# Order of the four TensorE products in a unit of two feature blocks: high, low, high, low or high, high, low, low

## The chip, the cores and the metric

The kernel runs on one core of a Trainium2 chip. The metric is the device time of one execution in microseconds (us). A core has a matrix engine (TensorE, PE in the profile, with its weight loads listed as PEld), a vector engine (DVE), a scalar engine (ACT), GpSimd (POOL) and a queue engine (SP) that issues the transfers from HBM. PE writes its results into PSUM, which has banks of 512 fp32 values in each of 128 partitions.

## The reference, cut to what matters

Two layers act on 256 tokens of width 1024. Each layer is a SwiGLU block, a token mixer, and a second SwiGLU block:

```python
def swiglu(h, w_gate_up, w_down):
    a, b = jnp.split(h @ w_gate_up, 2, axis=-1)      # 1024 -> 2 x 2816
    return (jax.nn.silu(a) * b) @ w_down             # 2816 -> 1024

x = x + 0.5 * swiglu(rms_norm(x, ffn1_norm), ffn1_w_gate_up, ffn1_w_down)
h = rms_norm(x, mix_norm)
z = h @ w_in                                         # u, q, k, v and two gate logits of 1024
...                                                  # pooling, attention in one block of 256 positions
gates = jax.nn.sigmoid(gl + b_gate).reshape(B, S, N_BRANCH, D)
merged = gates[:, :, 0] * (y_pool @ w_branch_pool) + gates[:, :, 1] * (y_attn @ w_branch_attn)
x = x + merged @ w_out
x = x + 0.5 * swiglu(rms_norm(x, ffn2_norm), ffn2_w_gate_up, ffn2_w_down)
```

All of it is float32. What the change touches are the products `h @ w_gate_up` (four times) and the gate logits (twice).

## The kernel before, in words

**Split operands.** A float32 number is held as two float32r parts, a high one and a low one (the rest). A product of activations and weights is formed from three part products: weight-high by activation-high, weight-high by activation-low, and weight-low by activation-high. Activations lie features by tokens: `hx` has, for each block `k` of 128 features, a tile `hk[k]` of 128 x 2 x 256, whose first 256 columns are the high part and whose second 256 the low part. A block of weights is 128 x 128. So one matmul with a high weight block streams 512 columns (both parts, `prod` with `xk`), and one with a low weight block streams 256 (the high part alone, `xk[:, 0, :]`). Below, H is the first kind and L the second. Each matmul has its own weight load. `steps` only sets the order in which the columns of a matmul run.

**Weights.** They come from HBM in units of 128 x 2048 fp32 (16 blocks of 128 x 128, 1 MB), by `unit()`: SP issues the transfer into one of four `raw` buffers, ACT writes the high part (line 112) and DVE the low part (line 113), each in two halves of 8 blocks, into `hi` and `lo` tiles (six halves of each). ACT may overwrite a half when the matmuls that read it are done.

**A unit of two feature blocks.** `pair` makes two blocks of 128 output features (`j` = 0, 1) from one unit: `columns` runs over the eight blocks `k` of the contraction, and for each over `j`. The sums of `j` = 0 and `j` = 1 lie in two PSUM banks: `banks` gives a tile of 2 x 2 x 256 fp32 in each partition, and `ps[:, j]` is one bank of it, with the H product in both halves and the L product added onto the first half. For the first three units `pairs` runs the same `columns` in turns over pieces of `k`, one of the units with two `quarter` tiles in place of one `banks` tile (that is the list that `ps` can be). Two such `banks` tiles are in use by turns; `drain` adds the halves into SBUF (ACT, line 158, then DVE, line 159).

**Who calls it.** `ffn` calls `pair` (or `pairs`, or `columns` itself, in the first units) for the 22 units of `w_gate_up`, four times in all, and `gate` calls it for 8 units of gate logits in each of the two layers. That is 4 x 22 + 2 x 8 = 104 units of 8 blocks of `k`, 832 turns of the loop over `k`, and 1664 of H and as many of L. `chain` itself is also called by `project_u` and by the second half of `ffn` (the products by `w_down`, tiles `ga` and `gb`), one bank at a time; there its order is H, L, H, L. `tokens` (tile `pt`) alternates H and L as well, with activations as weights. `chain3`, in the mixer's later products and the last block of the output, uses matmuls of 256 columns alone: two with the high block and one with the low.

**Order.** All matmuls are kept in the order in which the program lists them (`keep`). The order within the other engines' queues is that of the program too.

Of the kernel before, what the change touches and what calls it, by code (L numbers as in the profile page):

```python
# [29 lines left out]
NK = D // P  # L30
# [19 lines left out]
def trunk_kernel(ctx: ExitStack, tc: tile.TileContext, x_in, w_in, pw_in, qkn_in, rope_in, mask_in, band_in, out):  # L50
# [28 lines left out]
    def mm(*args, **kw):  # L79
        return keep(nc.tensor.matmul(*args, **kw))  # L80
# [34 lines left out]
    def blk(z, b, n=1):  # L115

        c = b * P % HALF
        return z[b * P // HALF][:, c:c + n * P]

    def steps(z):  # L120

        if len(z.shape) == 3:
            z = z.rearrange("p a s -> p (a s)")
        return z.rearrange("p (s a c) -> p a s c", a=4, c=4)

    def prod(ps, w, xk, first, last):

        return mm(steps(ps), lhsT=w, rhs=steps(xk), start=first, stop=last)

    def chain(ps, hi, lo, b, xk, first, last):  # L130

        prod(ps, blk(hi, b), xk, first, False)
        return prod(ps[:, 0, :], blk(lo, b), xk[:, 0, :], False, last)
# [7 lines left out]

    def columns(w, ps, ks):

        for k in ks:
            for j in range(2):
                chain(ps[j] if isinstance(ps, list) else ps[:, j], *w, 2 * k + j, hk[k], k == 0, k == NK - 1)

    def pair(w, t, other=None, at=0):

        ps = banks(pmm, "ps")  # L150
        columns(w, ps, range(at))
        if other:
            other()
        columns(w, ps, range(at, NK))
        drain(t, ps)
# [5 lines left out]
    def pairs(ws, ts):  # L161

        pss = [banks(pmm, "ps"), banks(pmm, "ps"), [quarter("pe") for _ in range(2)]]
        for a, b in PIECES:
            for w, ps in zip(ws, pss):
                columns(w, ps, range(a, b))
        for t, ps in zip(ts[:2], pss):
            drain(t, ps)
        for j, pe in enumerate(pss[2]):
            act(ts[2][:, j, :], pe[:, 1, :], AF.Copy)  # L170
            tt(ts[2][:, j, :], pe[:, 0, :], ts[2][:, j, :], op=OP.add)
# [35 lines left out]
    hk = [hx[:, k] for k in range(NK)]  # L207
# [545 lines left out]
```

## Time and profile before

| what | value |
|---|---|
| runs | 1010.97 us median of 3 (1008.93, 1010.97, 1013.57) |
| profiled execution | span 1008.4 us from the first to the last instruction; no other time is given for it |
| PE busy | 1001.3 us, 99% of the span, 6348 matmuls and as many weight loads |
| PEld busy | 905.9 us |
| DVE busy | 795.9 us |
| ACT busy | 626.1 us |
| granted PE clock | 1.000 |

The profile has a page with the busy time of each engine, the chain of work that ended last and the costliest groups of instructions, and it can be asked for a timeline, for waits, and for groups in a window. "ps<-hx,hi" is a matmul that writes a tile `ps` from `hx` with a block of `hi`: an H of a unit of two feature blocks. A matmul's recorded duration (383 ns for 512 columns) includes the time to the end of its last write, while the next one has begun: for the rate of a row of matmuls the distance of the starts is read, not the duration.

### The profile page before, as it was taken

The numbers are of one execution on the slowest core, as the hardware profiler recorded it, in microseconds if no ns is written. First come the engines' busy times: TensorE is split into PE (matmuls) and PEld (weight loads), VectorE is DVE, ScalarE is ACT, GpSimd is POOL, SyncE is SP. The second block draws the span as 40 slices with busy tenths as digits, with TensorE's granted clock in tenths as the row PEclk, the third lists the DMA queues.
The fourth block names the chain that finished last, engine by engine and source line by source line (L and its number), as shares of the span: only waits on it lengthen the run. The fifth ranks groups of instructions, "written<-read, shape, count | busy, mean of one in ns | idle before, by whom it ended". The sixth has DMA issues, their size and how long they took to land.

```text
span 1008.4 us, 16031 instructions
## 1 busy us (share of the span) xinstructions
PE 1001.3 (99%) x6348; PEld 905.9 (90%) x6348; DVE 795.9 (79%) x1195; ACT 626.1 (62%) x985; POOL 1.4 (0%) x26
## 2 busy tenths in 40 slices
PE   8999999999999999999999999999999999999998
PEld 7889889898899998898898898898988998989987
DVE  7898866699769788886678888666998798888752
ACT  7966655567766766665576666556676567665641
POOL 0000000000000000000000000000000000000000
PEclk9999999999999999999999999999999999999999
DMA  8766566545526566656646565655544375656640
GB/s 290 272 229 218 180 209 209 192 156 169 204 84 227 192 209 209 209 174 206 206 168 211 206 209 175 207 203 186 189 167 147 118 255 173 228 181 209 207 148 22
DMA packets 30459, 192.91 MB, mean 191 GB/s; under 512 B 3376, under 2 KB 5680, under 8 KB 7856
## 3 DMA queue, kind: packets, MB, share of 16 engines
q1 hardware_dynamic: 30240, 191.71, 55.8%
q8 instruction: 50, 0.82, 0.3%
q10 hardware_dynamic: 144, 0.18, 0.1%
q14 instruction: 25, 0.20, 0.1%
HBM read 190.82 MB, written 1.05 MB: 190 GB/s over the span
## 4 chain that ended last, share of the span: by engine, by line
PE 84%; DVE 9%; ACT 3%; issue 2%; DMA 1%; SPq 0%; ACTq 0%; DVEq 0%
PE ps L80 73%; PE pt L80 6%; PE two L80 4%; DVE lo L113 3%; ACT hi L112 1%; DMA raw<-w 1%; DVE gates L159 1%; ACT pr L427 1%; DVE gates L483 1%; DVE nb L422 1%; DVE pr L432 1%; DVE sc L417 0%; ACT gates L486 0%; DVE gates L514 0%; DVE ab L322 0%
## 5 line engine op out<-in xcount | busy, mean ns | idle before, releaser
L80 PE MATMUL ps<-hx,hi 128*128 128x512 f32 x1712 | 574.8, 383 | 2.1 <-ACT hi L112 1.1
L113 DVE TENSOR_TENSOR lo<-raw,hi 128x1024 fp32r<-128x1024 f32 (+2 forms) x369 | 440.2, 1196 | 128.5 <-ACT hi L112 123.2
L112 ACT ACTIVATE hi<-raw 128x1024 fp32r<-128x1024 f32 (+2 forms) x369 | 379.3, 1035 | 219.0 <-PE ps L80 172.2
L80 PE MATMUL ps<-hx,lo 128*128 128x256 f32 x1712 | 467.8, 273 | 0.2 <-DVE lo L113 0.2
L80 PEld LDWEIGHTS ps<-hx,hi 128*128 128x128 f32 x1712 | 321.4, 188 | 60.9 <-DVE ab L159 1.7
L80 PEld LDWEIGHTS ps<-hx,lo 128*128 128x128 f32 x1712 | 321.7, 188 | 0.7 <-DVE lo L113 0.5
L80 PE MATMUL ps<-ga,hi 128*128 128x512 f32 (+1 forms) x528 | 172.4, 376 | 0.0
L80 PE MATMUL ps<-ga,lo 128*128 128x256 f32 x512 | 139.8, 273 | 0.0
L80 PEld LDWEIGHTS ps<-ga,hi 128*128 128x128 f32 x528 | 97.9, 188 | 16.6
L80 PEld LDWEIGHTS ps<-ga,lo 128*128 128x128 f32 x512 | 96.2, 188 | 0.0
L80 PE MATMUL ps<-gb,hi 128*128 128x512 f32 (+1 forms) x198 | 65.6, 376 | 0.0
L80 PE MATMUL pt<-hi,hx 128*128 128x512 f32 x192 | 65.1, 385 | 0.0
L322 DVE TENSOR_TENSOR ab<-ab,r 128x512 f32<-128x512 f32 x88 | 60.5, 691 | 2.4
L159 DVE TENSOR_TENSOR ab<-ps,ab 128x512 f32<-128x512 f32 x87 | 59.8, 687 | 2.2
L324 ACT ACTIVATE sg<-ab 128x256 f32<-128x256 f32 x88 | 36.6, 418 | 30.6 <-DVE ab L322 29.8
L80 PE MATMUL pt<-lo,hx 128*128 128x256 f32 x192 | 52.6, 274 | 0.0
L80 PE MATMUL ps<-gb,lo 128*128 128x256 f32 x192 | 52.4, 273 | 0.0
L158 ACT ACTIVATE ab<-ps 128x512 f32<-128x512 f32 x87 | 50.5, 580 | 0.3 <-PE ps L80 0.3
L175 ACT ACTIVATE ga<-sg 128x256 fp32r<-128x256 f32 x64 | 26.3, 418 | 36.4 <-DVE sg L325 35.2
L80 PE MATMUL two<-ax,hi 128*128 128x256 f32 x256 | 44.9, 278 | 0.1
L80 PE MATMUL ps<-ax,hi 128*128 128x256 f32 x256 | 44.1, 275 | 0.0
L80 PEld LDWEIGHTS ps<-gb,hi 128*128 128x128 f32 x198 | 36.7, 188 | 6.2
(148 smaller groups left out, 856.3 us busy)
## 6 DMA issues: line engine op xcount, KB each, us to landing
raw<-w SPq DMA_DIRECT2D x176, 1024.0 KB, 5.0
raw<-w SPq DMA_DIRECT2D x9, 256.0 KB, 6.2
raw<-w SPq DMA_DIRECT2D x2, 512.0 KB, 6.3
out_dram<-gx SPq DMA_DIRECT2D x8, 128.0 KB, 2.0
raw<-w SPq DMA_DIRECT2D x6, 128.0 KB, 3.7
gx<-x SPq DMA_DIRECT2D x3, 256.0 KB, 6.0
qk<-pw SPq DMA_DIRECT2D x2, 256.0 KB, 2.7
qkn<-qkn SPq DMA_DIRECT2D x1, 256.0 KB, 5.4
```

Of the source, the lines that this page charges most:

```text
L80: return keep(nc.tensor.matmul(*args, **kw))
L112: act(hi, w, AF.Copy)
L113: tt(lo, w, hi.bitcast(F32), op=OP.subtract)
L158: act(t, ps[:, :, 1, :], AF.Copy)
L159: tt(t, ps[:, :, 0, :], t, op=OP.add)
L175: act(d[:, 0, :], v, AF.Copy)
L322: tt(ab, ab, bc2(r[0]), op=OP.mult)
L324: act(sg, ab[:, 0, :], AF.Silu)
L422: nc.vector.tensor_reduce(nb[:, j, :], sc[:, :, c], axis=AX.X, op=OP.max)
L427: act(pr[:, h, c], sc[:, h, c], AF.Exp, scale=DH ** -0.5, bias=nb[:, j, h:h + 1], accum_out=su[:, j, h:h + 1])
L432: tt(pr[:, :, c], pr[:, :, c], su[:, j, :].unsqueeze(2).to_broadcast([P, 2, n]), op=OP.mult)
L483: tt(gates[:, f], gates[:, f], bc2(r), op=OP.mult)
```

## The change

In `columns` alone, the four matmuls of a block `k` change their order. Before: H of `j` = 0, L of `j` = 0, H of `j` = 1, L of `j` = 1. After: H of `j` = 0, H of `j` = 1, L of `j` = 0, L of `j` = 1. So two H follow each other, then two L, and every matmul writes to the other bank than the one before it. The number of matmuls, weight loads, their shapes and operands stay the same; `start` and `stop` flags stay on the same matmuls (the first H and the last L of each bank).

```diff
     def columns(w, ps, ks):
 
+        hi, lo = w
+        pj = ps if isinstance(ps, list) else [ps[:, j] for j in range(2)]
         for k in ks:
             for j in range(2):
-                chain(ps[j] if isinstance(ps, list) else ps[:, j], *w, 2 * k + j, hk[k], k == 0, k == NK - 1)
+                prod(pj[j], blk(hi, 2 * k + j), hk[k], k == 0, False)
+            for j in range(2):
+                prod(pj[j][:, 0, :], blk(lo, 2 * k + j), hk[k][:, 0, :], False, k == NK - 1)
```

## The prediction

> **What bounds the kernel now.** I read the page first: span, busy shares, the chain of work that ended last, the costliest groups.
>
> ```profile
> span 1008.4 us, 16031 instructions
> ...
> PE 1001.3 (99%) x6348; PEld 905.9 (90%) x6348; DVE 795.9 (79%) x1195; ACT 626.1 (62%) x985; POOL 1.4 (0%) x26
> ...
> PEclk9999999999999999999999999999999999999999
> ...
> PE 84%; DVE 9%; ACT 3%; issue 2%; DMA 1%; SPq 0%; ACTq 0%; DVEq 0%
> ...
> L80 PE MATMUL ps<-hx,hi 128*128 128x512 f32 x1712 | 574.8, 383 | 2.1 <-ACT hi L112 1.1
> ...
> L80 PE MATMUL ps<-hx,lo 128*128 128x256 f32 x1712 | 467.8, 273 | 0.2 <-DVE lo L113 0.2
> ```
>
> PE is busy nearly all the time, at full granted clock, and makes up 84% of the chain. The busy time says little of its rate, since matmuls overlap: the two bottom rows hold H (512 columns) and L (256 columns), 383 and 273 ns long each. Their idle time, 2.1 and 0.2 us in all, says that PE hardly waits for anybody. So the kernel lasts as long as its matmuls need at their rate, and the change touches that rate alone. Hence I read the chain in order of time for rates over long stretches, and the timeline for single starts.
>
> ```profile
> 46.57 139.22 PE ps L80 x832
> 185.79 10.96 PE pt L80 x64
> ...
> 208.21 10.68 PE pt L80 x64
> ...
> 339.11 176.00 PE ps L80 x1056
> ```
>
> Columns: start in us, length in us, what, count. 176.00 us for 1056 matmuls, H and L by turns, is 333.3 ns for an H and an L together. This stretch holds both the units of two blocks and the products by `w_down`. Before 46.57 us the chain runs through DMA, ACT and DVE too; after it, nearly all is PE. The two `pt` rows come in below.
>
> ```profile
> 500.17 0.28 PE L80 MATMUL ps<-ga,lo 128*128 128x256 f32 x1
> 500.28 0.38 PE L80 MATMUL ps<-ga,hi 128*128 128x512 f32 x1
> 500.50 0.27 PE L80 MATMUL ps<-ga,lo 128*128 128x256 f32 x1
> 500.61 0.38 PE L80 MATMUL ps<-ga,hi 128*128 128x512 f32 x1
> 500.83 0.28 PE L80 MATMUL ps<-ga,lo 128*128 128x256 f32 x1
> ...
> 500.17 0.19 PEld L80 LDWEIGHTS ps<-ga,hi 128*128 128x128 f32 x1
> 500.28 0.19 PEld L80 LDWEIGHTS ps<-ga,lo 128*128 128x128 f32 x1
> 500.50 0.19 PEld L80 LDWEIGHTS ps<-ga,hi 128*128 128x128 f32 x1
> ```
>
> The timeline (start, length). An L begins 0.22 us after an H, an H 0.11 us after an L; of the 333.3 ns I give 221 to the H and 112 to the L. Each weight load begins with the matmul ahead of its own (500.28 H, 500.28 load of the next L): loads run one ahead, no further. Under an H a load of 0.19 us recorded has 221 ns; under an L it has 112, less than its recorded length, and yet the next H starts on time, so its end is recorded late, as with matmuls.
>
> **The change, part by part.** Nothing is added or removed: 832 groups H L H L become H H L L. Each of the four pairs of neighbours has a price, the distance from the first's start to the second's. Before: two of H to L, two of L to H, 2 x 333.3 = 666.7 ns. After: H to H, H to L, L to L, L to H.
>
> H to L and L to H keep 221 and 112 ns. Whether the bank changes between two matmuls has shown no price: the `ga` rows above stay in one bank, while from L to H of a unit of two blocks the bank changes, and there it is 0.11 us too (514.50 to 514.61):
>
> ```profile
> 514.50 0.27 PE L80 MATMUL ps<-hx,lo 128*128 128x256 f32 x1
> 514.61 0.38 PE L80 MATMUL ps<-hx,hi 128*128 128x512 f32 x1
> 514.83 0.28 PE L80 MATMUL ps<-hx,lo 128*128 128x256 f32 x1
> 514.95 0.39 PE L80 MATMUL ss<-ar,one_r 128*128 128x256 f32 x2
> 515.18 0.39 PE L80 MATMUL ps<-hx,hi 128*128 128x512 f32 x1
> 515.41 0.28 PE L80 MATMUL ps<-hx,lo 128*128 128x256 f32 x1
> 515.52 0.38 PE L80 MATMUL ps<-hx,hi 128*128 128x512 f32 x1
> 515.74 0.28 PE L80 MATMUL ps<-hx,lo 128*128 128x256 f32 x1
> 515.86 0.39 PE L80 MATMUL ps<-hx,hi 128*128 128x512 f32 x1
> ```
>
> H to H stands nowhere in the trace. The nearest row is H to L, also a stream of 512 columns under which the load of the next has ample room: 221 ns. Bounds: the slow `pt` row below, 342.5 for H and L, leaves at most 342.5 - 112 = 230; at the other end I allow twice the shortest time that an L could take, 2 x 109 = 218 (the 109 comes with the loads below).
>
> L to L does stand in the trace: `chain3` has 256 columns only.
>
> ```profile
> L80 PE MATMUL ps<-ax,lo 128*128 128x256 f32 x52 | 14.3, 275 | 0.0
> ...
> 309.75 0.28 PE L80 MATMUL ps<-ax,lo 128*128 128x256 f32 x1
> ...
> 327.29 0.28 PE L80 MATMUL ps<-ax,lo 128*128 128x256 f32 x1
> ```
>
> These are the group of one window and its first and last row. One matmul in three has a low block; 52 of them span 51 threes, 17.54 us, so 343.9 ns for three and 114.6 for one. That is 2.6 ns over the 112 of an L ahead of an H, and with no engine to blame: no idle time stands in the row. I take 114.6 for L to L, and 112 for L to H, since there the next matmul is an H as it was. The `ss` row above agrees: three 256-column matmuls in a row, 514.83 to 515.18, take 0.35 us.
>
> The sum for a group is 221 + 221 + 114.6 + 112 = 668.6 against 666, and in differences + 2.6 ns. What a short matmul allows its successor's load bounds it from below:
>
> ```profile
> 218.62 0.90 PEld L399 LDWEIGHTS tp<-ident,q 128*128 128x128 f32 x8
> ```
>
> Eight loads back to back, the last recorded at about 0.14: (0.90 - 0.14) / 7 = 109 ns each. A load needs nearly what an L gives it, so two L in succession have no slack to share, and no order gets a load for less than 109. The Trainium skill, "TensorE: Matmul & The Clock Gate", section "LDWEIGHTS (loading the stationary operand)", gives columns / 1.2, an estimate of 107 ns for 128; its "Back-to-back issue gap" gives N / 2.4 + 2.5, 216 and 109 ns. By that page a group costs 650 ns in either order, no change, while the trace has 667.
>
> Times 832 groups: + 2.2 us. Groups before 46.57 us are covered: at 5.3 us a unit (16 x 333.3 ns) nine units or 72 groups at most, and PE waits there for others anyway.
>
> ```profile
> PE ps L80 <- ACT hi L112: 1.1, 1, 1.1
> PEld ps L80 <- DVE ab L159: 1.7, 3, 0.8
> ...
> PE ps L80 <- DVE lo L113: 0.2, 1, 0.2
> ...
> 11.85 0.38 PE L80 MATMUL ps<-hx,lo 128*128 128x256 f32 x1 [0.24 <-DVE lo L113]
> ...
> 40.62 0.50 PE L80 MATMUL ps<-hx,hi 128*128 128x512 f32 x1 [0.46 <-DVE ab L159]
> ```
>
> The waits name who ended PE's idle time. At 11.85 us an L waits for DVE's low part; after the change both H run ahead of it, so 0.22 us of work moves out of the way, and it is lost again at 40.62 us, where PE waits for DVE to free a bank. If that cover were gone it would be worth 0.3 us. So the term is 760 x 2.6 = 2.0 us, on the path that sets the end.
>
> The rest costs nothing. The queues of SP, ACT and DVE keep their instructions and order. Each group's last matmul is still the L of `j` = 1, so a half unit of `hi` and `lo` is released at the same point or 0.1 us earlier, and ACT, which waits for PE and not PE for ACT, hides it. The H of `j` = 1 is wanted 0.11 us earlier than before, and `hi` is written a unit ahead. `drain` starts after the same last matmul.
>
> Against the profiled execution this is 1008.4 + 2.0 = 1010.4 of span; its runs' median stands 2.6 us above that span, and I carry those over: 1010.97 + 2.0 = 1013.0 us.
>
> **The rivals.** *Slower: a slow rhythm.* The two `pt` rows are the same 64 matmuls with the same shapes, and one set takes 10.96 us, the other 10.68: 342.5 and 333.8 ns for H and L. The first set keeps its slow rhythm to its end, with PE waiting for nobody. So the rate depends on how the starts fall against something periodic, not on operands alone. Three short matmuls in a row upset it: after the `ss` rows the next H to H distances are 0.34 us (515.18 to 515.52 to 515.86), not 0.333. The new order puts two L in a row into every group. If each throws PE into the slow rhythm, a group costs 2 x 342.5 = 685 ns, 18.3 more, 13.9 us in 760 groups: 1024.9. It decides (over 0.5%, about what a measurement of this kernel can tell from no change, 5.05 us) from 6.6 ns per group on, a third of that. Against it: nearly all H and L of the trace find back to 333 by themselves, and the short row at 309.75 costs only 2.6 ns each. Chance 0.28, with everything between.
>
> *Faster: slack shared out.* If PE could use the room under the two H to load further ahead, or if H and L of one bank in succession now pay for touching the same sums, alternation saves it. The floor for the L is the load's 109: 2 x (112 - 109) = 6 ns; for two H, 2 x (221 - 218) = 6. Half to all of 12 ns x 832 is 5 to 10 us, so 1001 to 1006. Against it: loads start with the matmul ahead and no sooner, and banks show no price from L to H. The page named above (section "Step-by-step: what each phase is for") says that a window of 64 instructions pulls loads ahead of matmuls in flight; the load rows at 500.28 and 500.50 show one load ahead, which leaves it little. Chance 0.17.
>
> *Nothing happens.* H to H 221, both L 112: the same 666.7 ns, 1011.0. It lies within my forecast's own range.
>
> **How the numbers follow.** Forecast, with its own range of 0 to 5.2 ns a group (none to both L at 114.6, 1011 to 1015): 0.55. Slow rhythm 0.28, slack 0.17. The range runs from the middle of the faster case to the end of the slower one: 1004 to 1025. These are also the chances of within 0.5%, slower and faster by more.
>
> **What would show it.** In the changed kernel the timeline of a unit should read H, 0.22, H, 0.22, L, 0.115, L, 0.11, H; the chain's long `ps` rows 334 ns for two matmuls in the units (unchanged in `w_down`); idle time ahead of `ps` rows as now. L to L of 0.12 with H at 0.225 would be the slow rhythm; 0.109 or H to H below 0.22 the slack. The prediction is wrong if H to H has a price of its own, since no row of this trace holds one.

## The result, and the profile after

The changed kernel takes 1020.61 us (median of 3 runs, 1020.31 to 1021.68) against 1010.97 before: ratio 1.0096, interval 1.0067 to 1.0124. That is slower, by more than the 0.5% that the prediction took for noise. The profiled execution took 1021.68 us, with a span of 1019.4 us, 11.0 us longer than before.

First the page of the changed kernel (busy shares; shares of the chain that ended last, by engine; two groups):

```profile
PE 1006.7 (99%) x6348; PEld 909.2 (89%) x6348; DVE 792.4 (78%) x1195; ACT 620.1 (61%) x985; POOL 1.5 (0%) x26
...
PE 66%; DVE 21%; ACT 6%; issue 5%; DMA 1%; SPq 0%; DVEq 0%
...
L328 ACT ACTIVATE sg<-ab 128x256 f32<-128x256 f32 x88 | 36.5, 417 | 91.1 <-DVE ab L326 90.9
...
L80 PE MATMUL ps<-gb,hi 128*128 128x512 f32 (+1 forms) x198 | 66.5, 379 | 5.4 <-DVE gb L180 5.4
```

PE's busy share still reads 99%, but PE's share of the chain fell from 84% to 66%, and DVE's rose from 9% to 21%. The idle time in the last row is new: in the product by `w_down` PE waits 5.4 us, four times in all, for `gb`, the last results of SwiGLU. ACT now waits 91 us for DVE's `ab`, where it was 30.

PE's rate inside the units did not change. The timeline inside a unit (a row with x2 holds two matmuls):

```profile
600.39 0.60 PE L80 MATMUL ps<-hx,hi 128*128 128x512 f32 x2
600.83 0.39 PE L80 MATMUL ps<-hx,lo 128*128 128x256 f32 x2
601.05 0.60 PE L80 MATMUL ps<-hx,hi 128*128 128x512 f32 x2
```

From one pair of H to the next, 600.39 to 601.05, is 0.66 to 0.67 us, two H in 0.44 and two L in 0.22. Over a long stretch the chain in order of time gives the same; here are its rows of the changed kernel, and one of the kernel before that the prediction does not show:

```profile
189.40 10.96 PE pt L80 x64
...
342.73 72.03 PE ps L80 x432
...
691.36 10.72 PE pt L80 x64
```

```profile
683.36 10.96 PE pt L80 x64
```

72.03 us for 432 matmuls is 333.5 ns for an H and an L, 667.0 for a group of four; before it was 666.7. The `pt` rows are where the mixers begin. The first begins 3.6 us later than before (189.40 against 185.79). The whole mixer, with 64 groups of the changed order, lasts as long as before: 189.40 to 342.73 is 153.33 us, 185.79 to 339.11 was 153.32. The two SwiGLU blocks between the mixers take 348.63 us instead of 344.25, 4.4 more. From the second mixer to the end it is 328.0 instead of 325.0. So the loss lies in the SwiGLU blocks, about 3 us in the first, 2.2 in each of the middle two, 3 in the last. A lower clock does not explain it: the granted clock of the two profiled executions is 1.000 before and 0.998 after, and the kernel with H H L L and the old queues, below, has 0.998 too and loses nothing.

What DVE and ACT do there is the key. First DVE and then ACT in the first SwiGLU block of the changed kernel (the lines of `columns` moved the later code by 4: `drain` is 162 and 163, the norm `ab` 326, Silu 328, its product 329, the split `ga` or `gb` 179 and 180):

```profile
123.43 0.69 DVE L326 TENSOR_TENSOR ab<-ab,r 128x512 f32<-128x512 f32 x1
...
127.03 1.23 DVE L113 TENSOR_TENSOR lo<-raw,hi 128x1024 fp32r<-128x1024 f32 x1 [0.52 <-ACT hi L112]
128.17 0.68 DVE L163 TENSOR_TENSOR ab<-ps,ab 128x512 f32<-128x512 f32 x1
128.89 0.69 DVE L326 TENSOR_TENSOR ab<-ab,r 128x512 f32<-128x512 f32 x1
129.50 1.22 DVE L113 TENSOR_TENSOR lo<-raw,hi 128x1024 fp32r<-128x1024 f32 x1
130.63 0.42 DVE L329 TENSOR_TENSOR sg<-sg,ab 128x256 f32<-128x256 f32 x1
131.53 0.43 DVE L180 TENSOR_TENSOR gb<-sg,gb 128x256 fp32r<-128x256 f32 x1 [0.48 <-ACT gb L179]
...
134.34 0.69 DVE L326 TENSOR_TENSOR ab<-ab,r 128x512 f32<-128x512 f32 x1
```

```profile
125.63 0.42 ACT L179 ACTIVATE gb<-sg 128x256 fp32r<-128x256 f32 x1 [0.99 <-DVE sg L329]
125.95 1.04 ACT L112 ACTIVATE hi<-raw 128x1024 fp32r<-128x1024 f32 x1
...
131.08 0.42 ACT L179 ACTIVATE gb<-sg 128x256 fp32r<-128x256 f32 x1 [0.99 <-DVE sg L329]
131.40 1.04 ACT L112 ACTIVATE hi<-raw 128x1024 fp32r<-128x1024 f32 x1
```

From one `ab` to the next is 5.455 us (123.43, 128.89, 134.34), while PE needs 8 groups x 667 ns = 5.336 us for a unit. The brackets (idle time and who ended it) show why nobody catches up. ACT writes `gb`, and only behind it, in its queue, the next `hi`. That `hi` releases DVE's `lo`, behind which stand `drain`, `ab`, the other `lo` and `sg`; and `sg` releases ACT's next `gb`. It is a closed ring: 125.63 to 125.95 to 127.03 to 128.17 to 128.89 to 129.50 to 130.63 to 131.08, which is 0.32 + 1.08 + 1.14 + 0.72 + 0.61 + 1.13 + 0.45 = 5.45 us. No wait in it is for PE.

PE does not feel the difference of 0.12 us at once. It works from `hi` and `lo` that lie ready: the row 342.73 above, at the start of the second block, holds 72 us at 333.5 ns for an H and an L, while the ring turns in most of it. The lag of ACT and DVE grows meanwhile, and PE meets most of it at the end of each block, in the four waits for `gb` of up to 1.4 us. (In the first block it loses part of the lag earlier, unit by unit.)

In the kernel before the same engines went through two units by turns (DVE, then ACT):

```profile
112.73 0.69 DVE L322 TENSOR_TENSOR ab<-ab,r 128x512 f32<-128x512 f32 x1
113.34 1.22 DVE L113 TENSOR_TENSOR lo<-raw,hi 128x1024 fp32r<-128x1024 f32 x1
114.48 0.42 DVE L325 TENSOR_TENSOR sg<-sg,ab 128x256 f32<-128x256 f32 x1
114.92 1.23 DVE L113 TENSOR_TENSOR lo<-raw,hi 128x1024 fp32r<-128x1024 f32 x1
116.06 0.42 DVE L176 TENSOR_TENSOR gb<-sg,gb 128x256 fp32r<-128x256 f32 x1
```

```profile
113.84 1.04 ACT L112 ACTIVATE hi<-raw 128x1024 fp32r<-128x1024 f32 x1
114.93 0.42 ACT L175 ACTIVATE gb<-sg 128x256 fp32r<-128x256 f32 x1
116.38 1.06 ACT L112 ACTIVATE hi<-raw 128x1024 fp32r<-128x1024 f32 x1 [1.03 <-PE ps L80]
```

Here ACT writes a `hi` ahead of `gb` in every second unit, DVE's `lo` needs not wait behind `gb`, and ACT ends up waiting for PE (1.03 us): PE sets the pace.

So the queues of ACT and DVE came out in another order, 160 places of 937 on ACT and 231 of 1195 on DVE, though the change does not touch them. Only the matmuls are held in the program's order (`keep`); a planner orders the other engines when the kernel is built. How it chooses was not looked into; the order of the matmuls is all that differs between the two kernels, so its choice depends on that. The section on the kernel before says that the other queues follow the program; that is wrong.

### The profile page after: what moved, and what is told of

It is laid out like the page before. It is cut to its first block, busy times and chain, and to the rows that moved or that the text cites. A ratio compares the mean times of both kernels' runs of the same rounds, so it can differ in the third digit from the quotient of the medians.

```text
span 1019.4 us, 16071 instructions
## 1 busy us (share of the span) xinstructions
PE 1006.7 (99%) x6348; PEld 909.2 (89%) x6348; DVE 792.4 (78%) x1195; ACT 620.1 (61%) x985; POOL 1.5 (0%) x26
## 4 chain that ended last, share of the span: by engine, by line
PE 66%; DVE 21%; ACT 6%; issue 5%; DMA 1%; SPq 0%; DVEq 0%
PE ps L80 52%; DVE lo L113 14%; PE pt L80 7%; ACT hi L112 5%; PE two L80 4%; DVE ab L163 3%; DVE sg L329 2%; DVE ab L326 1%; PE sc L80 1%; DMA raw<-w 1%; PE pt L443 1%; PE pe L80 0%; PE tp L403 0%; DVE ga L180 0%; SPq L648 0%
## 5 line engine op out<-in xcount | busy, mean ns | idle before, releaser
L113 DVE TENSOR_TENSOR lo<-raw,hi 128x1024 fp32r<-128x1024 f32 (+2 forms) x369 | 439.6, 1195 | 127.2 <-ACT hi L112 125.9
L80 PE MATMUL ps<-hx,hi 128*128 128x512 f32 x1712 | 524.2, 385 | 2.7 <-ACT hi L112 2.3
L80 PE MATMUL ps<-hx,lo 128*128 128x256 f32 x1712 | 335.5, 273 | 0.0
L80 PEld LDWEIGHTS ps<-hx,hi 128*128 128x128 f32 x1712 | 259.5, 189 | 6.2 <-ACT hi L112 2.5
L180 DVE TENSOR_TENSOR ga<-sg,ga 128x256 fp32r<-128x256 f32 x64 | 26.7, 423 | 22.7 <-ACT ga L179 22.7
```

The costliest lines, as they stand in the source:

```text
L113: tt(lo, w, hi.bitcast(F32), op=OP.subtract)
L180: tt(d[:, 1, :], v, d[:, 0, :].bitcast(F32), op=OP.subtract)
```

## The experiments

Two theories stood against each other. *Queues*: the time comes from the new order of ACT and DVE. *Rhythm*: H H L L costs PE more, the slower rival of the prediction. Since the queues can be written out, each can be had without the other: a list of the issue order is added to the kernel, and each instruction of the engine is put behind the one ahead of it in the list, without a wait.

```python
for a, b in zip(order, order[1:]):      # order: places in the program, for ACT and for DVE
    tc.add_manual_dep(every[b], every[a].name, info_no_sync, reason="in_order")
```

The list moves the code down by 98 lines: line 80 is 178 in these kernels, 112 and 113 are 210 and 211.

**H H L L with the old queues.** The changed kernel with the lists of the kernel before.

> The changed order of the matmuls (H H L L), with the instructions of ACT and DVE issued in exactly the order that they had in the kernel before. Queue theory (the time went up because ACT's and DVE's queues came out in another order): ratio to before 0.998 to 1.003, no wait of PE for the last SwiGLU tiles. Rhythm theory (H H L L itself costs PE more): ratio 1.007 to 1.012, as the changed kernel.

Measured: 1009.71 us, ratio 0.9994 (0.9983 to 1.0005). The loss is gone, and with it the wait for `gb`. The longest wait of PE's weight loads:

```profile
PEld ps L178 <- ACT hi L210: 1.9, 1, 1.9
```

**H L H L with the new queues.** The kernel before with the lists of the changed one.

> The matmul order of before (H L H L), with ACT and DVE in exactly the order that they have in the changed kernel. Queue theory: ratio to before 1.007 to 1.012, with four waits of PE of about 1.4 us for DVE's last SwiGLU tile (gb). Rhythm theory: ratio 0.998 to 1.003.

Measured: 1022.18 us, ratio 1.0107 (1.0089 to 1.0125). The same waits:

```profile
PEld ps L178 <- DVE gb L274: 6.5, 4, 1.7
PEld ps L178 <- DVE ab L257: 2.0, 11, 0.3
```

The whole loss, without the changed order of matmuls, with four waits for `gb`. In both directions the time goes with the queues.

**Control.** The kernel before with its own lists.

> Control: the kernel before, with its own order of ACT and DVE written out. Both theories: ratio to before 0.998 to 1.002; anything else is a cost of writing the order out.

Measured: 0.9999 (0.9985 to 1.0012). Writing the order out costs nothing.

**One swap in ACT's queue.** In the changed kernel's own lists, ACT's `hi` goes ahead of the `ga` or `gb` before it.

```diff
 ACT:  silu
-      ga (line 179)
       hi (line 112)
+      ga
       drain, hi, silu ...
```

> The changed kernel with its own queues, but in ACT's queue each first write of a half of SwiGLU's result (line 179, ga and gb) that stands directly ahead of a high part of weights (line 112) changes places with it (85 places). Loop theory (ACT and DVE wait for each other in a closed ring of 5.455 us a unit, longer than PE's 16 x 333.3 ns = 5.333 us): the ring loses about 0.5 us, PE sets the pace again, ratio to before 0.998 to 1.003. Rhythm theory: stays at 1.007 to 1.012. If the order of DVE's queue alone matters: 1.007 to 1.012 too.

Measured: 1015.6 us, ratio 1.0049 (1.0034 to 1.0064): half of the loss, which neither theory had said. The waits show part of the rest:

```profile
PEld ps L178 <- DVE gb L278: 1.7, 4, 0.4
PEld ss L178 <- DVE ar L278: 0.8, 3, 0.3
```

The swap had also hit the sum of squares `ar`, which PE needs at once, and the last unit of a block, where PE is about to read `gb` and ACT now first waits for a free `hi`. So it was made again, at the 67 places inside the rings alone; besides the places named, ten that stand ahead of the rings at the start of the blocks are left out.

> As the one-swap kernel, but only at the 67 places inside the rings: the sum of squares (ar) that a swap had held up, and the last unit of each block, keep their places. Ring theory: what the first swap left over was the price of those places; ratio to before 0.998 to 1.002. Otherwise, if the ring isn't all of it: 1.003 to 1.005 as with all 85.

Measured: 1009.88 us, ratio 0.9988 (0.9973 to 1.0003). ACT in the steady part:

```profile
116.17 0.42 ACT L426 ACTIVATE sg<-ab 128x256 f32<-128x256 f32 x1 [0.65 <-DVE ab L424]
117.13 1.06 ACT L210 ACTIVATE hi<-raw 128x1024 fp32r<-128x1024 f32 x1 [0.54 <-PE ps L178]
118.09 0.40 ACT L277 ACTIVATE gb<-sg 128x256 fp32r<-128x256 f32 x1
...
122.46 1.06 ACT L210 ACTIVATE hi<-raw 128x1024 fp32r<-128x1024 f32 x1 [0.54 <-PE ps L178]
```

From `hi` to `hi` is now 5.33 us, and ACT waits for PE: the ring is open. Exchanging 67 neighbouring pairs in one queue removes the loss, with DVE's order as in the changed kernel.

**A shorter ring.** The order stays as in the changed kernel, and one link of the ring goes out.

```diff
-                tt(ab, ab, bc2(r[0]), op=OP.mult)
```

> The changed kernel with its own order of ACT and DVE, without DVE's multiplication of each unit by the norm (ab by r, 0.61 us from start to start, 88 of them; the output is not the reference's). Ring theory: the ring shrinks from 5.455 to about 4.85 us a unit, under PE's 5.333, so the loss goes without any change of order: ratio to before 0.996 to 1.001, no wait for gb. If the order itself costs, whatever the ring's length: 1.006 to 1.011.

Measured: 1009.44 us, ratio 0.9983 (0.9970 to 0.9996). DVE's `drain` starts at:

```profile
111.62 0.68 DVE L257 TENSOR_TENSOR ab<-ps,ab 128x512 f32<-128x512 f32 x1
...
116.96 0.68 DVE L257 TENSOR_TENSOR ab<-ps,ab 128x512 f32<-128x512 f32 x1
```

5.34 us, PE's pace, in the order that had lost 1%. The order is not dear by itself; it is dear because its ring is longer than PE's unit.

**Half the dose.** The new lists in the first and third SwiGLU block only.

> H H L L; ACT and DVE in the order of before, but in two of the four SwiGLU blocks (the first and the third) in the order of the changed kernel. Queue theory, each block's ring losing by itself: half of the loss, ratio to before 1.003 to 1.006, with two of the four waits for gb, in those two blocks. If the loss came from one place (the start, or one block): near 1.000 or near 1.010.

Measured: 1016.28 us, ratio 1.0055 (1.0033 to 1.0077), with two waits for `gb` (3.3 us on the weight loads). So the loss goes by the block.

**Which queue.** H H L L with one list of the changed kernel and one of the kernel before.

> H H L L; ACT in the order of the changed kernel, DVE in that of before. Ring theory (the place of ACT's high part of weights behind its part of SwiGLU's result closes the ring): a loss as in the changed kernel or a good part of it, 1.005 to 1.012. If DVE's order is what counts: 0.998 to 1.003.

> H H L L; DVE in the order of the changed kernel, ACT in that of before. Ring theory: ACT has its high part ready early in every second unit, so at most a part of the loss, 0.998 to 1.005. If DVE's order is what counts: 1.007 to 1.012.

Measured: with the new ACT list 1009.18 us, 0.9983 (0.9970 to 0.9996), against what the ring theory had expected here; with the new DVE list 1109.5 us, 1.0984 (1.0958 to 1.1010), far above what either said. Both expectations took one queue for the cause. A ring needs both. With DVE's old list `lo` stands ahead of `gb` in every second unit, and in this run that opens the ring although ACT has the new list: ACT waits for PE again. With DVE's new list and ACT's old one a longer ring closes; DVE's row, two units apart, and one of ACT's between:

```profile
100.81 1.23 DVE L211 TENSOR_TENSOR lo<-raw,hi 128x1024 fp32r<-128x1024 f32 x1 [1.00 <-ACT hi L210]
...
104.86 1.23 DVE L211 TENSOR_TENSOR lo<-raw,hi 128x1024 fp32r<-128x1024 f32 x1 [1.49 <-ACT hi L210]
...
113.79 1.22 DVE L211 TENSOR_TENSOR lo<-raw,hi 128x1024 fp32r<-128x1024 f32 x1 [1.00 <-ACT hi L210]
```

```profile
103.46 0.42 ACT L426 ACTIVATE sg<-ab 128x256 f32<-128x256 f32 x1 [2.68 <-DVE ab L424]
103.79 1.04 ACT L210 ACTIVATE hi<-raw 128x1024 fp32r<-128x1024 f32 x1
```

ACT's `hi` now also stands behind Silu, which waits 2.68 us for DVE. Two units take 12.98 us (100.81 to 113.79), 6.49 each, 1.16 over PE's 5.33, and no link between those two rows waits for PE. Here PE does wait inside the block, 65 times for DVE's `drain`. For some 70 units 1.16 us is 81 us; with the waits for `gb` at the ends (19.6 us on the weight loads) that is an estimate of 101 us, where the medians differ by 98.6.

**Is a little gained?** The kernel with the new ACT list and the old DVE list was run again beside its twin with H L H L.

> H H L L with ACT's order of the changed kernel and DVE's of before, a second time, beside its twin with H L H L. If it is really a little faster than before: 0.997 to 0.9995; else 0.9995 to 1.001.

> The matmul order of before (H L H L) with ACT's order of the changed kernel and DVE's of before: the twin of the H H L L kernel with the same two orders, which came out at 0.9983. If that small gain is the queues': 0.997 to 0.9995 here too. If it is H H L L's: 0.999 to 1.001 here.

Measured: 0.9985 (0.9972 to 0.9997) and, for the twin, 0.9992 (0.9978 to 1.0006). The H H L L version came out 0.15% below the kernel before, twice, with intervals that end just under 1, and 1.1% below the changed one. Whether H H L L or the queues brings that 0.15% stays open; the twins' intervals overlap.

## Why the prediction was right, and where it was wrong

The time lay within the range and on the side of the forecast, but that was luck. It rose by 9.6 us where 2.0 were forecast; it fell into the case that had 0.28 and not into the likeliest; and the range reached so far up only for a slow rhythm of PE, which is not what made the loss.

*The sum for a group held, its one term did not.* A group is 667.0 ns where 668.6 was forecast and 666.7 stood before. In the trace of H H L L with the old queues, averaged over the units between 345 and 455 us, H to H is 223 ns, H to L 220, L to L 113 and L to H 110, where 221, 221, 114.6 and 112 were forecast. So L to L does take 3 ns more than L to H, but the pairs beside it give it back; the prediction changed one price and left the others as they were. On its own, with the old queues, the new order gives 0.9994, at most + 0.5 us and at least - 1.7: the + 2.0 us did not come. Two banks by turns, or one bank, made no difference to the sum.

*The rivals about PE.* No slack was shared out. The slow rhythm did not take hold in the units (333.5 ns over a whole stretch, not 342.5). It did once elsewhere, in the last product by `w_down`, whose order H L H L the change leaves alone, from the wait for `gb` to the end:

```profile
962.65 53.36 PE ps L80 x332
...
979.86 0.39 PE L80 MATMUL ps<-ga,hi 128*128 128x512 f32 x1
...
981.92 0.39 PE L80 MATMUL ps<-ga,hi 128*128 128x512 f32 x1
```

The first row is of the chain, the others of the timeline. Six H and L take 2.06 us, 343 ns each where the same product takes 333 in the kernel before. Averaged from 964 us to the end it is 342.2; over 132 of them that costs 1.2 us. The traces of three other kernels with waits for `gb` (H L H L with the new queues, the first swap, half the dose) have it in the third block's product, about 1.4 us each. In these products of the kernels without such waits it does not occur, but neither does it in the kernel with the longest waits (the new DVE list). What sets it off is not shown, nor that anything periodic stands behind it.

*The step that failed* is "The queues of SP, ACT and DVE keep their instructions and order", and with it "The rest costs nothing". SP's did; ACT's and DVE's did not. The cover was thin too: the prediction let ACT and DVE follow PE, since PE hardly waited for them and ACT waited for PE, and it did not ask how much later they might be before that turns. In the new order a turn of the ring through both takes 5.455 us, where PE needs 5.336. The excess, 0.119 us for each of the 67 units whose places were swapped, is 8.0 us of the 11.0 that the span grew. The slow rhythm at the end is 1.2 more. About 1.1 us lies at the start and is not the rings': with H H L L and the old queues the first mixer also begins at 186.91 instead of 185.79, and PE's wait for the first `hi` is 1.8 us there, 2.3 in the changed kernel and 1.1 before. The 0.7 us that remain were not taken apart.

*Was it to be seen before?* Partly. In the trace of before the order of DVE's rows is not that of the program, which lists `drain` and the next unit's `lo` apart from the SwiGLU of an older unit; in the rows above `lo` stands between `ab` and `sg`. That says that something reorders, and then a change of PE's order can change any queue. Which order it would give, and that its ring would be too long, could not be read from the trace of before.

## What to carry to other kernels

Where a planner sets the order of some queues, an edit to one engine's order can be an edit to all: compare the issue order of every engine before explaining a time, and write the old order out to test the edit alone. Busy shares hide a ring: two engines at 78% and 61% can set the pace if their waits for each other close, so add up the links from start to start and hold the sum against the bound engine's period. The ring here was opened by one kind of swap, or by one shorter link, and changing one queue of a pair alone can close a worse one (here 9.8%).

## What the runs showed of the hardware

TensorE ran two 512-column matmuls and two 256-column ones, each with its own weights, in 667 ns in either order, in one bank or by turns in two. A row of H and L by turns ran at 333 ns for the two in most places and at 342 in some, to the end of the row and with PE waiting for nobody. Most of what PE lost it lost to lateness of 2% in ACT and DVE (5.455 against 5.336 us a unit), which came out as 1% of the whole time.
